# Layer A of a two-layer trunk: plain products for the in-projection, convolution and gate straight from PSUM

## The chip, the cores and the metric

The kernel runs on one core of one Trainium2 chip. Five engines work side by side: TensorE multiplies matrices (the profile writes PE, and PEld for its weight loads), VectorE (DVE), ScalarE (ACT) and GpSimd (POOL) work element by element, and SyncE (SP) issues most of the DMAs. Each engine runs its own instructions in order and waits on semaphores for the others. SBUF is the working memory of 128 partitions; matmuls write their results to PSUM, from where DVE or ACT fetch them.

The metric is the device time of one execution in microseconds (us), the median of several executions. The profile is of one further execution; its span runs from the first to the last instruction.

## The reference

The input x has 2048 tokens of 1024 features. Two layers follow, each `x <- x + mixer(rmsnorm(x))`, and a final norm. Layer A is a recurrent mixer, layer B a gated short convolution; both widen 1024 features to 1536 channels (12 heads of 128), with a SiLU gate beside them:

```python
def rg_lru(u, gate_w, gate_b, lam):
    g = sigmoid(einsum('bshi,hio->bsho', u by heads, gate_w) + gate_b)
    r, i = halves of g
    log_a = -LRU_C * r * softplus(-lam)
    a = exp(log_a)
    bterm = sqrt(-expm1(2 * log_a)) * (i * u)
    return h with h[t] = a[t] * h[t-1] + bterm[t]

def recurrent_mixer(h, w_in, conv_w, conv_b, gate_w, gate_b, lam, w_out):
    u = h @ w_in
    gate, xb = u[..., :WIDTH], u[..., WIDTH:]
    xb = causal_depthwise_conv(xb, conv_w, conv_b)     # 4 taps
    y = rg_lru(xb, gate_w, gate_b, lam)
    return (y * silu(gate)) @ w_out

def shortconv_mixer(h, w_in, conv_w, w_out):
    bg, cg, xv, gate = four parts of h @ w_in
    y = bg * causal_depthwise_conv(cg * xv, conv_w)    # 3 taps
    return (y * silu(gate)) @ w_out
```

(The code above is shortened from the reference.) Everything is float32.

## The kernel before

**Products.** A float32 product is made of three float16 matmuls (`mm3`, L475, L478 and L479 in the profile): operands are split into a high and a low half. For activations `add` does it (L280 on ACT, L282 on DVE, tiles `op`), for weights `split` inside the in-projection (L400 on ACT, L401 on DVE, tiles `wc`, eight buffers), and `OutProj.split` for the out-projections (L1029, L1030, tiles `zs` and `wf`). Products accumulate in PSUM in six tiles tagged `acc`; two more PSUM tiles, tagged `g`, hold gates and small sums. The split weights are scaled by a power of two, and `undo` takes the scale back at the eviction.

**Units.** The in-projection of a layer goes by units of 256 output channels (two heads, m = 0 and 1). Layer A has 12 units, two for each pair of heads: an x unit (the recurrent branch) and a g unit (the gate). Each unit runs over two halves of 1024 tokens, each of two chunks c of 512. A half-unit is a 2 by 2 block product: `unit` computes it by Winograd's scheme with seven products of 12 matmuls (PSUM tiles p, q and r), `unit_of_blocks` with eight. In layer A units 0 and 1 go by blocks (the first chunk of unit 0 even in float32, `first_blocks`), units 2 to 11 by Winograd, and so does all of layer B.

Winograd needs sums of operands: T1 to T4 of the activations (`build_sums`: L306 on POOL and DVE) and S1 to S4 of the weights (`wsum`: L452 on POOL), so a unit has seven split weight tiles. Its results come out one after another, each computed from an earlier one (`plus`, L514 on DVE; copies L524 and L540 on ACT). `unit_weights` is the preparation of the next unit's weights: load (L389), squares for the scale (L362), the scale itself (L371 to L380), then the splits. It is a generator that is advanced a step at a time between the products of the present unit (`pace`).

**The mixer of layer A** is a generator too, one for each pair, half and chunk, advanced from the list `side`. For each of the two heads: the convolution (first tap L761 on POOL or L757 on ACT, three more L768 on DVE) reads `xb` from SBUF, where three columns before the chunk were copied by `halos` (L195, L198). Two gate matmuls in float32 follow (L783, two records each), tanh (L787), exp and tanh (L794, L795), a square (L796), two products on DVE (L797, L800). One root over both heads (L806, which needs another activation table), then the product on POOL (L812), the scan on DVE (L813), its last column (L817), the product with the gate on POOL (L819, which makes z in the tile `sg`), the store of z to DRAM (L686) and its square for the scale of the out-projection (L690). The gate itself comes from the g unit: tanh (L845) and a DVE step (L848). `u`, `th`, the tanh tiles and `a` share nine buffers `e`.

**Order.** In a pair, x half 0, x half 1, g half 0 and g half 1 follow one another. The mixer of half 0, chunk 0 is started after x half 1, that of chunk 1 after g half 0, those of half 1 after g half 1; so a pair's mixers run while its g unit and the next pair's x unit are computed. For the last pair all but the first mixer are marked `late`: they have their own tiles and run inside the out-projection, held behind its products (`hold`). The final order on each engine is laid out by a scheduler before the run, from the order of the program, `tc.high_priority` and order-only edges (`after`).

**The out-projection** (`OutProj`) loads z back (`zr`), splits it, and computes each output tile from 12 heads. It begins with the first five pairs of chunk 0 (`EARLY`), so that the last pair has time.

**Layer B's gate** is tanh (L939), a DVE step (L940) and a product on POOL (L944); the factor 0.5 that this form of SiLU needs is put into the convolution's weights (`bwh`).

## Time and profile before

| | us |
|---|---|
| median of 3 runs | 2152.18 |
| lowest and highest | 2148.42, 2154.61 |
| profiled execution | 2150.58 |
| its span | 2148.8 |

The stages, read off PE's timeline: the start with units 0 and 1 up to 157.8 us; units 2 to 11 of layer A up to 686.75; the out-projection of layer A from 693.2 to 982.7; layer B from there, its out-projection in the last 270 us. A row of a group gives the line in the source, the engine, the operation, what it writes and reads, and after the bar its busy time in us, the mean ns of one, and the idle time of that engine just before it with what ended most of it.

### The profile page before, as it was taken

Reading aid. Unit: us, or ns where it says so; the run is one execution under the profiler, and the core shown is the slowest. Engines: PE = TensorE matmul, PEld = TensorE weight load, DVE = VectorE, ACT = ScalarE, POOL = GpSimd, SP = SyncE. Lnnn points to the kernel's source line nnn. Section 1 sums busy time; section 2 is a strip of 40 time slices with the busy share of each in tenths; the row PEclk is TensorE's granted clock in tenths of the full one; section 3 lists DMA queues with packets and bytes.
Section 4 is the critical chain, followed back from the end, with each engine's and each line's share of the span. In section 5 each row is a group of like instructions: output and inputs, shape, how many; then the busy total and the mean of one; then the engine's idle time right before and its main releaser. Section 6 shows DMA issues by size and latency. Waiting matters only on the chain.

```text
span 2148.8 us, 25164 instructions
## 1 busy us (share of the span) xinstructions
PE 1979.2 (92%) x9110; PEld 924.0 (43%) x9110; DVE 1375.4 (64%) x2058; ACT 997.1 (46%) x1833; POOL 809.0 (38%) x650
## 2 busy tenths in 40 slices
PE   7587898989788979998899999999999999999997
PEld 3232343434233434443344444444444444444467
DVE  8679787878668763747974653744736547465323
ACT  6456777776657563314343333342442332344221
POOL 3644453545433131325553342433442423313220
PEclk9798999999899989998999999999999999999999
DMA  5101121121311435442102112121120020193202
GB/s 190 43 5 45 59 74 64 60 89 45 104 48 50 167 129 131 167 108 69 41 29 89 40 35 79 34 74 42 43 98 30 33 81 5 66 346 132 85 23 71
DMA packets 94205, 167.74 MB, mean 78 GB/s; under 512 B 11456, under 2 KB 15168, under 8 KB 94080
## 3 DMA queue, kind: packets, MB, share of 16 engines
q1 hardware_dynamic: 93520, 164.82, 23.5%
q0 software_dynamic: 560, 1.32, 0.3%
q8 instruction: 71, 1.16, 0.2%
q14 instruction: 54, 0.44, 0.1%
HBM read 124.14 MB, written 41.96 MB: 77 GB/s over the span
## 4 chain that ended last, share of the span: by engine, by line
PE 61%; DVE 21%; ACT 8%; DMA 5%; issue 4%; POOL 1%; SPq 0%; DVEq 0%; ACTq 0%; POOLq 0%
PE acc L478 6%; PE acc L479 6%; PE acc L475 6%; PE q L479 6%; PE q L475 6%; PE q L478 6%; DVE u L768 4%; PE p L475 4%; PE p L478 4%; PE p L479 4%; PE r L479 4%; PE r L475 4%; PE r L478 4%; DVE tg L813 3%; DVE op L282 3%
## 5 line engine op out<-in xcount | busy, mean ns | idle before, releaser
L475 PE MATMUL q<-op,wc 128*128 128x512 f16 x816 | 310.8, 382 | 21.7 <-DVE xb L514 6.4
L475 PEld LDWEIGHTS <-wc 128*128 128x128 f16 x2016 | 201.6, 100 | 293.9 <-ACT wc L400 36.9
L479 PEld LDWEIGHTS <-wc 128*128 128x128 f16 x2016 | 199.6, 99 | 290.8 <-issue 55.4
L478 PEld LDWEIGHTS <-wc 128*128 128x128 f16 x2016 | 199.4, 99 | 273.1 <-issue 50.1
L475 PE MATMUL acc<-zs,wf 128*128 128x512 f16 (+1 forms) x864 | 304.1, 359 | 13.6 <-ACT zs L1029 10.4
L478 PE MATMUL acc<-zs,wf 128*128 128x512 f16 (+1 forms) x864 | 308.4, 357 | 4.5 <-DVE zs L1030 4.3
L478 PE MATMUL q<-op,wc 128*128 128x512 f16 x816 | 311.8, 382 | 0.4 <-DVE op L282 0.4
L479 PE MATMUL q<-op,wc 128*128 128x512 f16 x816 | 311.5, 382 | 0.0
L479 PE MATMUL acc<-zs,wf 128*128 128x512 f16 (+1 forms) x864 | 306.8, 357 | 0.0
L475 PE MATMUL p<-op,wc 128*128 128x512 f16 x544 | 209.2, 385 | 23.5 <-ACT wc L400 22.9
L475 PE MATMUL r<-op,wc 128*128 128x512 f16 x544 | 208.1, 383 | 9.8 <-ACT wc L400 6.5
L478 PE MATMUL r<-op,wc 128*128 128x512 f16 x544 | 208.1, 383 | 8.8 <-DVE op L282 8.8
L478 PE MATMUL p<-op,wc 128*128 128x512 f16 x544 | 209.2, 385 | 0.0
L479 PE MATMUL p<-op,wc 128*128 128x512 f16 x544 | 208.6, 384 | 0.7 <-DVE wc L401 0.7
L479 PE MATMUL r<-op,wc 128*128 128x512 f16 x544 | 207.4, 381 | 1.3 <-DVE fixed L817 1.2
L401 DVE SCALAR_TENSOR_TENSOR wc<-ws,fixed,wc 128x512 f16<-128x512 f32 x140 | 141.5, 1018 | 93.5 <-ACT wc L400 92.8
L217 POOL TENSOR_TENSOR sa<-sa,sq 128x512 f32<-128x512 f32 x70 | 99.9, 1428 | 213.6 <-ACT sq L216 145.6
L890 POOL TENSOR_TENSOR pb<-pb,cg 128x512 f32<-128x512 f32 x48 | 65.8, 1371 | 242.9 <-ACT pb L540 162.0
L452 POOL TENSOR_TENSOR ws<-wr 128x512 f32<-128x512 f32 x70 | 110.2, 1574 | 94.0 <-ACT pre L713 33.9
L768 DVE SCALAR_TENSOR_TENSOR u<-xb,fixed,u 128x512 f32<-128x512 f32 x144 | 129.8, 923 | 2.9 <-POOL u L761 2.8
L475 PEld LDWEIGHTS <-wf 128*128 128x128 f16 x864 | 85.4, 99 | 97.3 <-issue 9.8
L783 PE MATMUL pg<-u,gts 128*128 128x512 f32 x192 | 100.5, 633 | 24.0 <-DVE u L768 9.3
(188 smaller groups left out, 3269.5 us busy)
## 6 DMA issues: line engine op xcount, KB each, us to landing
wr<-in_wb SPq DMA_DIRECT2D x100, 256.0 KB, 3.2
xs<-in_xT SPq DMA_DIRECT2D x48, 256.0 KB, 5.7
zA<-sg SPq DMA_DIRECT2D x48, 256.0 KB, 2.0
zr<-zA SPq DMA_DIRECT2D x48, 256.0 KB, 5.3
zB<-ed SPq DMA_DIRECT2D x48, 256.0 KB, 2.0
zr<-zB SPq DMA_DIRECT2D x48, 256.0 KB, 5.3
wr<-in_wa SPq DMA_DIRECT2D x44, 256.0 KB, 3.6
xr<-x SPq DMA_DIRECT2D x32, 256.0 KB, 5.2
```

The lines of the kernel that those rows point to most:

```text
L217: squared[0] = eng.tensor_tensor(out=acc, in0=acc, in1=sq, op=ALU.add)
L282: return hi, v.tensor_tensor(out=t[:, 1, :], in0=src, in1=t[:, 0, :], op=ALU.subtract)
L401: v.scalar_tensor_tensor(out=t[:, 1, :], in0=src, scalar=sw[:, 2:3], in1=t[:, 0, :], op0=ALU.mult, op1=ALU.subtract,)
L452: g.tensor_tensor(out=t, in0=x, in1=y, op=op)
L475: ins = nc.tensor.matmul(acc, wh, xh, start=start, stop=False, **kw)
L478: nc.tensor.matmul(acc, wh, xl, start=False, stop=False, **kw)
L479: return nc.tensor.matmul(acc, wl, xh, start=False, stop=stop, **kw)
L768: v.scalar_tensor_tensor(out=u, in0=tap(k), scalar=wc(k), in1=u, op0=ALU.mult, op1=ALU.add)
L783: ins = nc.tensor.matmul(pg, gw[m][:, oo], u, start=True, stop=True)
L813: v.tensor_tensor_scan(out=y, data0=a, data1=w, initial=stA[:, h : h + 1], op0=ALU.mult, op1=ALU.add,)
L890: g.tensor_tensor(out=t, in0=t, in1=cg[m, half, c], op=ALU.mult)
```

## The change

1. **Plain products.** Units 2 to 11 of layer A go by `unit_of_blocks` too. `unit_weights` then makes four splits and no sums; `build_sums` and its calls are gone. Layer B stays with Winograd.
2. **Convolution from PSUM.** `unit_of_blocks` hands its accumulators to an `evict` function. For x units that is `conv`: ACT makes the last tap with the bias, DVE adds three shifted taps, all reading PSUM, and three columns are kept in a small `tail` tile for the next chunk, whose first columns get three small steps. There are no halos in layer A. The taps are scaled by `undo`. `u` takes one of the eight `xc` buffers.
3. **Gate from PSUM.** For g units `evict` is `silu`: tanh on ACT and one step on DVE, both reading PSUM, into `sg`.
4. **Mixers.** Those of a half start right after the x half. They have no convolution in them, work in place in `u`, and the `late` forms are gone: the last pair is treated like the others.
5. **z when both factors are there.** `gate` is called after the scan and after the silu; the later of the two makes z, on DVE instead of POOL, and issues its store. The square of z is emitted four steps later (`defer`, `tick`), behind the last product, into a tile of its own (`zjunk`); this holds for layer B too.
6. **Layer B's gate** is one `AF.Silu` on ACT; the DVE step and `bwh` go.

```diff
+        if plain:
+            for name, a in (("A11", a11), ("A21", a21), ("A12", a12), ("A22", a22)):
+                w[name] = split(a, sw)
+                yield
+            return
...
-    def unit_of_blocks(w, ops, dest, done, end, chunks=range(2)):
+    def unit_of_blocks(w, ops, dest, done, end, chunks=range(2), evict=None, pin=False):
...
+                        if pin:
+                            pe_last[0] = blocks_last[0]
                 if kh == 0:
+                    flush()
                     yield
             for m in range(2):
+                if evict:
+                    evict(m, c, accs[m], w["undo"])
+                    continue
...
-            take(n, 0, w, prep, False, pace=SCALE)
-            take(n, 1, w, prep, False)
+            take(n, 0, w, prep, plain(n), pace=[0, 0, 1, 0, 0] if plain(n) else SCALE)
+            take(n, 1, w, prep, plain(n))
...
+            def conv(m, half, c, a, undo=None):
+                h = heads[m]
+                us[m, half, c] = u = xct("u")[:, 0:CH]
...
+                with tc.high_priority(1000):
+                    s.activation(u, a, AF.Identity, scale=ac(3), bias=col(PC_AB + h))
+                    for n in range(1, 4):
+                        v.scalar_tensor_tensor(
+                            out=u[:, n:], in0=a[:, 0 : CH - n], scalar=ac(3 - n), in1=u[:, n:],
                             op0=ALU.mult, op1=ALU.add,
                         )
+                    v.tensor_scalar(
+                        out=tail[:, 0:3], in0=a[:, CH - 3 : CH],
+                        scalar1=1.0 if undo is None else undo, scalar2=None, op0=ALU.mult,
+                    )
+                    for n in range(1, 4) if before is not None else ():
                         v.scalar_tensor_tensor(
+                            out=u[:, 0:n], in0=before[:, 3 - n : 3], scalar=wc(3 - n),
+                            in1=u[:, 0:n], op0=ALU.mult, op1=ALU.add,
                         )
...
+            def gate(m, half, c):
+                if (m, half, c) in gated and (m, half, c) in scanned:
+                    z = sg[m, half, c]
+                    v.scalar_tensor_tensor(
+                        out=z, in0=us[m, half, c], scalar=gu[1], in1=z, op0=ALU.mult, op1=ALU.mult
+                    )
+                    store_z("A", hp, m, half, c, z)
+                    z_square(z, hp, m, half, c)
...
-                for m, (h, a, w, y, thi) in enumerate(kept):
-                    g.tensor_tensor(out=w, in0=w, in1=thi, op=ALU.mult)
+                for m, (h, a, w, u) in enumerate(kept):
+                    g.tensor_tensor(out=u, in0=w, in1=u, op=ALU.mult)
                     v.tensor_tensor_scan(
-                        out=y, data0=a, data1=w, initial=stA[:, h : h + 1],
+                        out=u, data0=a, data1=u, initial=stA[:, h : h + 1],
                         op0=ALU.mult, op1=ALU.add,
                     )
-                    v.tensor_copy(stA[:, h : h + 1], y[:, CH - 1 : CH])
-                    z = sg[m, half, c]
-                    g.tensor_tensor(out=z, in0=y, in1=z, op=ALU.mult)
-                    store_z("A", hp, m, half, c, z)
-                    z_square(z, y, hp, m, half, c)
+                    v.tensor_copy(stA[:, h : h + 1], u[:, CH - 1 : CH])
+                    scanned.add((m, half, c))
+                    gate(m, half, c)
...
             def xafter(half):
-                halos(xb, half, 3)
-                if half:
-                    side.extend([mixer(0, 0)] if hp else [mixer(1, 0), mixer(1, 1)])
-                    if hp == NH // 2 - 1:
-                        before_end(None)
+                side.extend([mixer(half, 0), mixer(half, 1)])
+                if half and hp == NH // 2 - 1:
+                    before_end(None)
...
+            def silu(m, half, c, a, undo):
...
+                sg[m, half, c] = t = sgt("sg")
+                with tc.high_priority(1000):
+                    s.activation(t, a, AF.Tanh, scale=gu[0][:, 0:1])
+                    v.scalar_tensor_tensor(
+                        out=t, in0=t, scalar=1.0, in1=a, op0=ALU.add, op1=ALU.mult
+                    )
                 gated.add((m, half, c))
+                gate(m, half, c)
...
             def gafter(half):
-                if half == 0:
-                    side.append(mixer(0, 1 if hp else 0))
-                    if hp == NH // 2 - 1:
-                        before_end(marks[-1])
-                else:
-                    side.extend([mixer(1, 0), mixer(1, 1)] if hp else [mixer(0, 1)])
+                if half == 0 and hp == NH // 2 - 1:
+                    before_end(marks[-1])
...
             def gdone(m, half, c, t):
                 th = et("th")
-                s.activation(th, t, AF.Tanh, scale=0.5)
-                v.scalar_tensor_tensor(
-                    out=th, in0=th, scalar=1.0, in1=t, op0=ALU.add, op1=ALU.mult
-                )
+                s.activation(th, t, AF.Silu)
```

`gu` holds half the unit's `undo` (for the tanh) and `undo` itself (for z), made by one small DVE step for each g unit.

More of the change, by code (lines that the diff above doesn't have):

```diff
@@ L143, in trunk @@
     gbh = keep(2 * NH)
-    bwh = keep(3 * NH)
     stA = keep(NH)
@@ L605, in first_done, with defer, tick @@
         return t
+    deferred = []
+    def defer(fn, steps):
+        deferred.append([steps, fn])
+    def tick(n=1):
+        for d in list(deferred):
+            d[0] -= n
+            if d[0] <= 0:
+                deferred.remove(d)
+                d[1]()
     def advance(side):
+        tick()
         while side and next(side[0], "end") == "end":
@@ L624, in take @@
         def take(n, half, w, prep, blocks, chunks=range(2), end=None, pace=None):
-            _, dest, done, before, after = units[n]
+            _, dest, done, before, after, *evict = units[n]
             before(half)
             pace = list(pace or ())
+            args = ()
+            if blocks:
+                take_out = evict and (lambda m, c, a, undo: evict[0](m, half, c, a, undo))
+                args = chunks, take_out, n > 1
             for _ in (unit_of_blocks if blocks else unit)(
                 w, ops[half], lambda m, c: dest(m, half, c), lambda m, c, t: done(m, half, c, t),
-                lambda: end(half) if end else after(half), *[chunks] * blocks
+                lambda: end(half) if end else after(half), *args
             ):
@@ L634, in take @@
                     next(prep, None)
-                for _ in range(1 + blocks + (l == 0 and half and n == len(units) - 1)):
+                for _ in range(1 + blocks):
                     advance(side)
@@ L638, in take, with plain @@
                 run(prep)
+        def plain(n):
+            return l == 0
         def start_blocks(w0, w1):
@@ L651, in ahead @@
             if n < len(units):
-                prep = unit_weights(l, units[n][0], w, behind=behind)
+                prep = unit_weights(l, units[n][0], w, behind=behind, plain=plain(n))
             next(prep, None)
@@ new lines, in conv, with wc, ac @@
+            def conv(m, half, c, a, undo=None):
+                h = heads[m]
+                us[m, half, c] = u = xct("u")[:, 0:CH]
+                if undo is not None and not taps:
+                    taps.append(cst.tile([P, 8], F32, tag="tap", name="tap", bufs=2))
+                    v.tensor_scalar(
+                        out=taps[0], in0=col(PC_AW + 8 * hp, 8), scalar1=undo, scalar2=None,
+                        op0=ALU.mult,
+                    )
+                def wc(k):
+                    return col(PC_AW + 4 * h + k)
+                def ac(k):
+                    return wc(k) if undo is None else taps[0][:, 4 * m + k : 4 * m + k + 1]
+                before = tails.get((m, 2 * half + c - 1))
+                tails[m, 2 * half + c] = tail = cst.tile([P, 4], F32, tag="tl", name="tl", bufs=8)
+                with tc.high_priority(1000):
[3 more added lines that the diff above has]
+                            out=u[:, n:], in0=a[:, 0 : CH - n], scalar=ac(3 - n), in1=u[:, n:],
@@ L776, in mixer @@
+            def mixer(half, c):
+                kept = []
                 for m in range(2):
-                    h = heads[m]
-                    u = us[m]
+                    if (half, c) == (0, 0):
+                        gw[m] = gate_weights(heads[m])
+                for m in range(2):
+                    h, u, w = heads[m], us[m, half, c], ws2[:, m, :]
                     th = []
@@ L807, in mixer @@
                 yield
-                yield
-                while any((m, half, c) not in gated for m in range(2)):
-                    yield
-                for m, (h, a, w, y, thi) in enumerate(kept):
-                    g.tensor_tensor(out=w, in0=w, in1=thi, op=ALU.mult)
+                for m, (h, a, w, u) in enumerate(kept):
+                    g.tensor_tensor(out=u, in0=w, in1=u, op=ALU.mult)
                     v.tensor_tensor_scan(
-                        out=y, data0=a, data1=w, initial=stA[:, h : h + 1],
+                        out=u, data0=a, data1=u, initial=stA[:, h : h + 1],
@@ L865, in in_A @@
+            def gafter(half):
+                if half == 0 and hp == NH // 2 - 1:
+                    before_end(marks[-1])
+            units.append((wa[2 * hp], xdest, nothing, beside, xafter, conv))
+            units.append((wa[2 * hp + 1], nothing, nothing, beside, gafter, silu))
         for hp in range(NH // 2):
@@ L1248, in second @@
         yield
-        behind = []
-        for ins in build_blocks(0, x1, inv1, hA[1]):
-            behind.append(ins[1])
-            yield
-        yield from build_sums(x0, hA[0], behind[NB])
+        yield from build_blocks(0, x1, inv1, hA[1])
     def ahead(l, wdram, sw=None):
```

114 lines of the change are left out of this document (31 added, 83 removed).

## The prediction

> **What bounds the kernel now.** I first read the page's engine totals and its 40 slices, to find the stages in which TensorE (PE) is not the limit.
>
> ```profile
> PE 1979.2 (92%) x9110; PEld 924.0 (43%) x9110; DVE 1375.4 (64%) x2058; ACT 997.1 (46%) x1833; POOL 809.0 (38%) x650
> ...
> PE   7587898989788979998899999999999999999997
> ...
> DVE  8679787878668763747974653744736547465323
> ...
> PEclk9798999999899989998999999999999999999999
> ```
>
> A slice is 53.7 us. From about slice 20 on PE is full, so layer B's in-projection and the last out-projection pay for matmuls alone. The holes are in the first 16 slices: layer A. I cut those stages with windows, at places taken from PE's timeline (the first product of unit 2, the last one of unit 11, the first and last matmuls of the out-projection).
>
> ```profile
> 157.80:688.60 530.80, 459.31 (x1871) 199.34 (x1869) 427.73 (x598) 368.65 (x637) 240.08 (x195) 0.95 0.20 64
> 693.20:982.70 289.50, 268.91 (x1213) 122.90 (x1213) 178.29 (x255) 125.30 (x216) 82.73 (x58) 0.96 0.45 135
> 982.70:1100.00 117.30, 100.75 (x448) 45.91 (x446) 102.29 (x145) 49.22 (x96) 65.12 (x48) 0.93 0.15 51
> ```
>
> The columns are span, then busy time of PE, weight load, DVE, ACT, POOL, then granted clock. In the 20 Winograd half-units (first row) PE is busy 459 of 531 us at a clock of 0.95, DVE 428. Next, PE's instruction groups in that window and, for the pace, its timeline.
>
> ```profile
> L475 PE MATMUL q<-op,wc 128*128 128x512 f16 x240 | 92.1, 384 | 12.2 <-DVE xb L514 6.4 <-DVE sg L514 5.7
> L783 PE MATMUL pg<-u,gts 128*128 128x512 f32 x168 | 84.4, 609 | 14.6 <-ACT wc L400 8.7 <-ACT th L845 2.9 <-DVE fixed L96 2.2
> L475 PE MATMUL p<-op,wc 128*128 128x512 f16 x160 | 62.9, 393 | 23.5 <-ACT wc L400 22.9 <-ACT sg L524 0.6
> L475 PE MATMUL r<-op,wc 128*128 128x512 f16 x160 | 62.7, 392 | 9.8 <-ACT wc L400 6.5 <-DVE fixed L817 3.3
> L478 PE MATMUL r<-op,wc 128*128 128x512 f16 x160 | 62.6, 391 | 8.8 <-DVE op L282 8.8
> ...
> L371 PE MATMUL pt<-fixed 128*128 128x4 f32 x18 | 2.5, 211 | 0.0
> ```
> ```profile
> 287.33 1.88 PE L783 MATMUL pg<-u,gts 128*128 128x512 f32 x4
> ...
> 686.75 1.88 PE L783 MATMUL pg<-u,gts 128*128 128x512 f32 x4
> 693.24 1.86 PE L475 MATMUL acc<-zs,wf 128*128 128x512 f16 x4 [4.61 <-ACT zs L1029]
> ...
> 949.67 0.38 PE L475 MATMUL acc<-zs,wf 128*128 128x512 f16 x1
> ...
> 965.85 0.38 PE L475 MATMUL acc<-zs,wf 128*128 128x512 f16 x1
> ```
>
> From the matmul at 949.67 to the one at 965.85 there are 75 starts: 16.18/75 = **0.2157 us** a matmul at full clock. A gate record (f32, two for each matmul) overlaps the next: (1.88 - 0.59)/3 = 0.43 us. So the in-projection, 157.8 to 686.75 = 529 us, holds 1680 x 0.2157 = 362 us of products, 168 x 0.43 = 72 us of gates and some 3 us of small matmuls: 438 us. **91 us are lost**: idle time, 71.5 us with the small groups not quoted, and about 20 us of lower clock behind it. The rows say what ended the idle time: weights (wc) 38.8 us with 0.7 in an unquoted row, evictions that a product accumulating on the same PSUM tile needs (xb, sg) 12.1, operands (op) 9.2. Only 11.4 us are anything else. DVE at 81% is late for all of these, but PE waits through them.
>
> **The change, part by part.** *Products.* A half-unit goes from 7 products of 12 matmuls to 8: +240 matmuls in the 20 half-units, 240 x 0.2157 = **+51.8 us** of PE. This cannot hide: PE is the busiest engine. With 184 gate records (the 8 that come before 157.8 stay there) the floor is 1920 x 0.2157 + 184 x 0.43 + 3 = 496 us.
>
> *Waits that go.* The plain unit splits four weight blocks and not seven, without the POOL sums, and takes 4 of the 8 wc buffers, so the next unit's four are made while this one runs: the 38.8 us on wc go. No product accumulates onto a tile that has been read half-way: the 12.1 us go. The operand sums T1 to T4 are not built any more: the 9.2 us on op go. The 11.4 us stay, with lower clock in their proportion, 20 x 11.4/71.5 = 3.
>
> *DVE, ACT and POOL.* These rows price the new work.
>
> ```profile
> L768 DVE SCALAR_TENSOR_TENSOR u<-xb,fixed,u 128x512 f32<-128x512 f32 x144 | 129.8, 923 | 2.9 <-POOL u L761 2.8
> ```
> ```profile
> L768 DVE SCALAR_TENSOR_TENSOR u<-xb,fixed,u x144: 718/744/1789, 91.9 to 763.9; 128x512 f32<-128x512 f32 x144
> ...
> L514 DVE SCALAR_TENSOR_TENSOR xb<-q,fixed,xb x30: 734/740/751, 196.2 to 661.1; 128x512 f32<-128x512 f32 x30
> ```
> ```profile
> L813 DVE TENSOR_TENSOR_SCAN tg<-a,fixed 128x512 f32<-128x512 f32 x40 | 73.1, 1830 | 3.0 <-POOL fixed L812 3.0
> ...
> L797 DVE SCALAR_TENSOR_TENSOR fixed<-fixed,tg 128x512 f32<-128x512 f32 x40 | 30.8, 770 | 21.5 <-ACT fixed L796 21.2
> ```
> ```profile
> L787 ACT ACTIVATE tg<-pg,fixed 128x512 f32<-128x512 f32 x82 | 53.1, 676 | 19.0 <-DVE fixed L817 6.4 <-PE q L479 6.3 <-PE p L479 3.6
> L794 ACT ACTIVATE a<-tg,fixed 128x512 f32<-128x512 f32 x41 | 33.2, 809 | 2.9 <-DVE tg L800 2.3 <-DMA zA<-sg 0.6
> ...
> L806 ACT ACT_TABLE_LOAD x20 | 25.7, 1283 | 0.3
> L690 ACT ACTIVATE tg<-sg 128x512 f32<-128x512 f32 x40 | 25.0, 624 | 86.3 <-DVE fixed L817 50.5 <-POOL sg L819 21.1 <-DVE fixed L96 13.0
> ...
> L806 ACT ACTIVATE fixed<-fixed 128x1024 f32<-128x1024 f32 x20 | 21.2, 1059 | 6.1 <-DVE fixed L797 6.0
> L400 ACT ACTIVATE wc<-wr,fixed 128x512 f16<-128x512 f32 x28 | 19.9, 711 | 14.3 <-DVE fixed L377 6.7 <-DVE tg L813 4.1 <-DVE sg L848 2.0
> ...
> L690 ACT ACTIVATION_READ_ACCUMULATOR tg<-sg 128x1 f32 x40 | 7.5, 188 | 0.0
> ...
> L757 ACT ACTIVATE u<-xb,fixed 128x512 f32<-128x512 f32 x4 | 3.2, 804 | 0.0
> ```
>
> The trace has no convolution from PSUM. The nearest row is the Winograd eviction (L514), which reads PSUM and one SBUF tile: 734 to 751 ns, never more. The present convolution (L768) reads two SBUF tiles: 744 ns at the median but up to 1789. I take 0.74 us; the other end, 0.92, is L768's mean. For 24 steps in a pair that is 4.4 us more of DVE.
>
> [...]
>
> For one pair of heads (four half-units, 97 us of PE) DVE then has 24 convolution steps x 0.74, 8 silu and 8 z products at 0.74, 16 mixer products at 0.77, 8 scans at 1.83, 8 splits near 0.8 and some 6 us of small columns: about 69 us, against 428 x 4/20 = 86 now. POOL keeps only the product before the scan. So DVE is not the bound on average.
>
> What is new is **crowding**. All mixers of an x half now run in the next half-unit: two in x half 1, two in g half 0, none in the others, where one per half-unit ran. ACT in x half 1: 8 gate tanh 5.4, 4 x (0.81 + 0.81 + 0.62) = 9.0, two roots 2.1, four table loads 5.1, 4 convolution starts at 0.8 = 3.2, 4 splits 2.8: 27.6 us. In g half 0: the same 21.6, plus 4 silu tanh 2.7, 8 squares with their accumulator reads 6.5: 30.8. Together 58.4 against PE's 2 x (96 x 0.2157 + 16 x 0.43) = 55.2. DVE, too, is full in x half 1: 12 convolution steps 8.9, 8 mixer products 6.2, 4 scans 7.3, 4 splits 3.2 and 3 of small columns, 28.6 against 27.6. ACT falls some 3 to 4 us behind in each pair and makes it up in g half 1. If PE waits for it, through the two gate PSUM tiles, that is 5 x 4 = 20 us; if the products go on, nothing. I take the middle, 10. So the in-projection loses 11.4 + 3 + 10 = 24 us: 496 + 24 = 520, **-9 us** against 529. Its bounds: 5 us lost (-28), and the present 91 (+58).
>
> *End of layer A.* Three of the last pair's four mixers now run inside the out-projection, on purpose held back. These are PE's groups in it.
>
> ```profile
> L478 PE MATMUL acc<-zs,wf 128*128 128x512 f16 x384 | 146.9, 383 | 4.5 <-DVE zs L1030 4.3
> ...
> L475 PE MATMUL acc<-zs,wf 128*128 128x512 f16 x384 | 142.6, 388 | 13.6 <-ACT zs L1029 10.4 <-DVE xr L1303 3.2
> L783 PE MATMUL pg<-u,gts 128*128 128x512 f32 x17 | 11.1, 782 | 7.0 <-DVE u L768 7.0
> ```
>
> From 686.75 to 982.7 are 296 us. 1152 x 0.2157 = 248.5, gates 17 x 0.43 = 7.3, small matmuls 5.7: 34.5 us are lost, 25 idle and the rest at low clock. After the change all mixers are done in g half 0, and z needs only the silu. The gates are counted above; the wait for u and for late z splits goes. What stays is the first wait, 4.6 + 1.2 us, and the cold clock behind it: I take 11 us in all. 265 against 296: **-31 us**; bounds 5 us lost (-37) and 30 (-12).
>
> *Start.* The last inverse norm lands here, and unit 2 begins there:
>
> ```profile
> 118.76 0.75 DVE L274 SCALAR_TENSOR_TENSOR xs<-xs,fixed,inv 128x512 f32<-128x512 f32 x1 [6.78 <-DMA inv<-rd]
> ```
> ```profile
> 157.83 0.38 PE L475 MATMUL p<-op,wc 128*128 128x512 f16 x1
> ```
>
> In these 39 us PE has 144 matmuls, 31 us, and a few gates. Without the operand sums about half the rest goes: **-3 us**, between -8 and +5, since more of pair 0's gates may fall there. Before 118 the chain is DMA and POOL squares, which the change leaves.
>
> *Layer B and the rest.* Silu saves 48 DVE steps under a PE that is full; I take -1 us, for the 983 to 1100 stretch, bounds 0 and -3. Deferred squares, the halo copies that go, and the tail columns lie beside PE: nothing; without that cover they belong to the crowding term. So do the head's gate weights: they are now asked for in the step whose matmul reads them, not two steps before.
>
> ```profile
> gts<-in_ga SPq DMA_DIRECT2D x12, 128.0 KB, 3.4
> ```
>
> If SP issues them no earlier, PE waits 3.4 us in each of five pairs, 17 us; I count nothing, since the slot of a head is free two pairs ahead and the order is laid out beforehand, and keep the 17 for the range. Weight loads and z stores share SP's queue; a store that waits for z holds the loads behind it, but a unit's load now has one whole unit (48 us) of slack.
>
> **Sum:** -9 - 31 - 3 - 1 = -44 us on a span of 2148.8. That execution took 2150.6; the median of the runs shown is 2152.2, so 2152 - 44 = **2108 us**.
>
> **The rivals.** (a) *Crowding in full*: PE waits the 20 us for ACT, wc waits stay at a third (13 us), and low clock behind them costs some 7 more. Lost 54 instead of 24: 2138. For it: ACT at 106% in two half-units of four. Against: the last wait before the products was rarely ACT's gates (2.9 us for th in the pg row). (b) *Everything hidden*: 5 us lost in the in-projection, 5 in the out-projection, start -8: 2108 - 19 - 6 - 5 = 2078. For it: layer B's in-projection, where PE is full at DVE's 40 to 80%. (c) *Slower*: the mixer chain (gate, exp, root, POOL product, scan) becomes the pace. u now lives from the convolution to z in eight buffers, a pair's full need; if four chains take longer than a pair of products, the next x half finds no u buffer, the six accumulators stay full and PE stops. Four chains in 97 us are 24 us each without cost; the forecast's pace is 520/20 = 26.0 us, and from 26.0 + 44/20 = 28.2 us a half-unit on, the whole gain is gone; with the present loss of 91 us the time is 2108 + 67 = 2175. For it: POOL's product now waits 92.1 us for the root (POOL group below). Against: what PE waited for was mostly not this, and in the second fence below a chain takes 17 us, from its first gate tanh at 513.02 to the end of its POOL products at 530.40.
>
> ```profile
> L812 POOL TENSOR_TENSOR fixed<-fixed,tg 128x512 f32<-128x512 f32 x38 | 56.4, 1504 | 101.3 <-ACT fixed L806 92.1 <-PE r L479 9.2
> ```
> ```profile
> 513.02 1.26 ACT L787 ACTIVATE tg<-pg,fixed 128x512 f32<-128x512 f32 x2
> ...
> 527.84 2.56 POOL L812 TENSOR_TENSOR fixed<-fixed,tg 128x512 f32<-128x512 f32 x2 [11.19 <-ACT fixed L806]
> ```
>
> **How the numbers follow.** Forecast 0.57 (its own range 2092 to 2125), (a) 0.17, (b) 0.15, (c) 0.11. The range 2080 to 2142 leaves out (c) and the outer edges. A measurement of this kernel tells about 0.3%, 6.5 us, from no change. Faster by more than that: 0.57 + 0.15 + most of (a) = 0.85; within: 0.05; slower: 0.10.
>
> **What would show it.** Right: the plain products of units 2 to 11 end about 520 us after they begin; no wait for wc above 10 us in all; convolution steps at 0.74 us with no 1.7 us cases; no gates in the out-projection, which takes about 265 us. Wrong: PE idle before gate records, or before acc products for want of u; table loads well above 48 in layer A; PE idle above 33 us in the in-projection, where its own saving is gone.

## The result and the profile after

| | before | after |
|---|---|---|
| median, us (4 runs each) | 2150.82 | 2075.07 |
| lowest and highest | 2148.42, 2154.61 | 2074.04, 2075.85 |
| span of the profiled execution | 2148.8 | 2073.5 |
| its granted clock | 0.967 | 0.984 |

After divided by before is 0.9646, with a 95% interval of 0.9629 to 0.9663: the kernel is 76 us faster. The forecast was 2108, the range 2080 to 2142. The direction was right, and so was the main reason: plain products take less time although they are more matmuls. But the gain is 1.7 times the 44 us that were forecast, and the time lies 5 us below the range: the terms for the loss that would stay, in the units and in the out-projection, were too large.

Engine totals and slices of after, from its page:

```profile
PE 2002.3 (97%) x9350; PEld 946.5 (46%) x9350; DVE 1194.3 (58%) x2047; ACT 962.6 (46%) x1756; POOL 567.2 (27%) x458
...
PE   6699999999999999988999999999999999999997
...
PEclk9899999999999999999999999999999999999998
```

The holes in the first 16 slices are gone. What is left is the start (two slices at 6), two slices at 8 where layer B begins, and the end. The stages, cut again at PE's first product of unit 2 (about 152 us), its last product of unit 11 (651.7) and the last matmul of the out-projection (904.3), by windows:

```profile
151.00:651.70 500.70, 495.86 (x2127) 225.10 (x2125) 338.04 (x677) 375.34 (x625) 54.85 (x45) 0.99 0.22 72
651.70:904.30 252.60, 252.60 (x1193) 117.12 (x1192) 133.92 (x189) 84.29 (x150) 63.07 (x44) 1.00 0.45 143
904.30:1050.00 145.70, 129.55 (x581) 59.00 (x580) 112.06 (x159) 60.49 (x118) 76.38 (x58) 0.94 0.13 41
```

PE is busy 495.86 of 500.70 us in the units at a clock of 0.99, and all of the 252.60 us of the out-projection at 1.00. The waits of PE in the units, which came to 71.5 us, are now two rows:

```profile
PE pg L820 <- ACT tg L824: 4.7, 1, 4.7
PE pt L722 <- ACT fixed L711: 0.2, 1, 0.2
```

| stage | before | after | measured | forecast |
|---|---|---|---|---|
| up to unit 2 | 157.8 | 152 | -6 | -3 |
| units 2 to 11 | 529 | 500 | -29 | -9 |
| to the end of the out-projection | 296 | 252.6 | -43 | -31 |
| layer B and the end | 1166.1 | 1169.2 | +3 | -1 |
| span | 2148.8 | 2073.5 | -75 | -44 |

Of the 31 us that the forecast lacked, 20 are in the units, 12 in the out-projection and 3 at the start; layer B took 4 back.

### The profile page after: what moved, and what is told of

Its sections match the earlier page's. It is cut to its first block, busy times and chain, and to the rows that moved or that the text cites. A ratio compares the mean times of both kernels' runs of the same rounds, so it can differ in the third digit from the quotient of the medians.

```text
span 2073.5 us, 25220 instructions
## 1 busy us (share of the span) xinstructions
PE 2002.3 (97%) x9350; PEld 946.5 (46%) x9350; DVE 1194.3 (58%) x2047; ACT 962.6 (46%) x1756; POOL 567.2 (27%) x458
## 4 chain that ended last, share of the span: by engine, by line
PE 80%; DVE 11%; DMA 3%; issue 3%; ACT 3%; POOL 1%; SPq 0%; DVEq 0%; ACTq 0%; POOLq 0%
PE acc L464 12%; PE acc L468 12%; PE acc L467 12%; PE q L468 6%; PE q L467 6%; PE q L464 6%; PE r L464 4%; PE p L468 4%; PE p L464 4%; PE p L467 4%; PE r L467 4%; PE r L468 4%; DVE op L280 3%; PE pg L820 2%; DVE xs L272 2%
## 5 line engine op out<-in xcount | busy, mean ns | idle before, releaser
L464 PEld LDWEIGHTS <-wc 128*128 128x128 f16 x2096 | 208.8, 100 | 277.6 <-issue 33.0
L468 PEld LDWEIGHTS <-wc 128*128 128x128 f16 x2096 | 206.2, 98 | 269.2 <-issue 25.9
L467 PEld LDWEIGHTS <-wc 128*128 128x128 f16 x2096 | 206.2, 98 | 265.0 <-issue 33.0
L464 PE MATMUL acc<-op,wc 128*128 128x512 f16 x752 | 283.7, 384 | 21.5 <-DVE sg L874 11.0
L467 PE MATMUL acc<-op,wc 128*128 128x512 f16 x752 | 287.1, 382 | 8.3 <-DVE op L280 8.2
L468 PE MATMUL acc<-op,wc 128*128 128x512 f16 x752 | 287.5, 382 | 2.9 <-DVE wc L385 2.9
L464 PE MATMUL q<-op,wc 128*128 128x512 f16 x576 | 218.4, 381 | 4.7 <-DVE pb L503 2.5
L468 PE MATMUL q<-op,wc 128*128 128x512 f16 x576 | 219.5, 381 | 0.0
L467 PE MATMUL q<-op,wc 128*128 128x512 f16 x576 | 219.2, 381 | 0.0
L845 POOL TENSOR_TENSOR u<-fixed,u 128x512 f32<-128x512 f32 x48 | 60.2, 1276 | 501.7 <-ACT fixed L842 501.7
L385 DVE SCALAR_TENSOR_TENSOR wc<-ws,fixed,wc 128x512 f16<-128x512 f32 x100 | 97.4, 975 | 98.3 <-ACT wc L384 98.3
L464 PE MATMUL p<-op,wc 128*128 128x512 f16 x384 | 146.3, 381 | 0.0
L467 PE MATMUL p<-op,wc 128*128 128x512 f16 x384 | 146.3, 381 | 0.0
L468 PE MATMUL p<-op,wc 128*128 128x512 f16 x384 | 146.0, 380 | 0.0
L468 PE MATMUL r<-op,wc 128*128 128x512 f16 x384 | 146.0, 380 | 0.0
L467 PE MATMUL r<-op,wc 128*128 128x512 f16 x384 | 146.0, 380 | 0.0
L464 PE MATMUL r<-op,wc 128*128 128x512 f16 x384 | 145.8, 380 | 0.0
```

Source lines behind the costliest of these rows:

```text
L385: v.scalar_tensor_tensor(out=t[:, 1, :], in0=src, scalar=sw[:, 2:3], in1=t[:, 0, :], op0=ALU.mult, op1=ALU.subtract,)
L464: ins = nc.tensor.matmul(acc, wh, xh, start=start, stop=False, **kw)
L467: nc.tensor.matmul(acc, wh, xl, start=False, stop=False, **kw)
L468: return nc.tensor.matmul(acc, wl, xh, start=False, stop=stop, **kw)
L845: g.tensor_tensor(out=u, in0=w, in1=u, op=ALU.mult)
```

## The experiments

Times are medians; the ratio is to the kernel before, run on the same chip. The kernel before took 2145 to 2149 us beside these runs (medians), so kernels are compared by ratio or on one chip.

| run | median us | ratio (95%) |
|---|---|---|
| e1_plain_only | 2089.37 | 0.9733 (0.9716 to 0.9749) |
| e6_plain_nolate | 2092.60 | 0.9749 (0.9724 to 0.9774) |
| e2_copy_first | 2072.85 | 0.9656 (0.9642 to 0.9671) |
| e3_mixers_later | 2072.34 | 0.9653 (0.9637 to 0.9669) |
| e12_more_steps | 2072.26 | 0.9650 (0.9635 to 0.9664) |
| e8_z_pool | 2074.25 | 0.9663 (0.9638 to 0.9688) |
| e4_tanh_b | 2070.39 | 0.9643 (0.9622 to 0.9664) |
| e5_act_3 | 2089.17 | 0.9735 (0.9719 to 0.9750) |
| e5_act_6 | 2119.90 | 0.9869 (0.9855 to 0.9884) |
| e7_wc14 | 2151.85 | 1.0024 (1.0011 to 1.0036) |
| e10_load_back | 2111.87 | 0.9831 (0.9817 to 0.9846) |
| e13_winograd_light | 2135.44 | 0.9919 (0.9898 to 0.9940) |
| e11_inv_pe | 2054.05 | 0.9561 (0.9545 to 0.9577) |
| e14_inv_pe_b | 2045.67 | 0.9510 (0.9494 to 0.9525) |
| e15_after_again | 2071.75 | 0.9631 (0.9616 to 0.9646) |

### Which part of the change carries the gain

**Plain products alone.** The kernel before with part 1 of the change and nothing else.

```diff
+        if plain:
+            for name, a in (("A11", a11), ("A21", a21), ("A12", a12), ("A22", a22)):
+                w[name] = split(a, sw)
+                yield
+            return
...
-            take(n, 0, w, prep, False, pace=SCALE)
-            take(n, 1, w, prep, False)
+            take(n, 0, w, prep, l == 0, pace=[0, 0, 1, 0, 0] if l == 0 else SCALE)
+            take(n, 1, w, prep, l == 0)
```

> The kernel before with one part of the change alone: units 2 to 11 of layer A by plain blocks (four weight splits, no operand or weight sums); convolution, gate, mixers and their places as before. Theory A (PE's losses in layer A came from the weight tiles, operand sums and Winograd's chained evictions, 60 of 71.5 us of idle time): PE waits in units 2 to 11 fall to about 10 to 15 us, these units take about 515 us against 529, the out-projection keeps its late mixers and its 296 us, the start gains 5; about 2130 us. Theory B (the losses came from DVE's load and the mixers' order, and Winograd only showed them): PE keeps 50 us or more of waits, the units take 550 us or more, 2165 us or more.

Measured: 2089.37 against 2146.37, so 57 us of the 76, and 41 below the 2130 of theory A. Its reason held, but the gain is larger on two counts: the units take 492 us (153.5 to 645.4) instead of its 515, and the out-projection, which it left at 296, takes 276. The last product of unit 11 starts at 645.2 us, 41 earlier than before (in after it is 35: seven us of the last pair's gates have moved ahead of it). The rest is lost between there and the end of the out-projection, which is at 921.5 and in after at 904.3. Windows of e1_plain_only, then of after, in the middle of that stage:

```profile
690.00:740.00 50.00, 38.25 (x152) 16.39 (x151) 40.36 (x63) 34.75 (x58) 18.68 (x13) 0.90 0.31 104
```
```profile
690.00:740.00 50.00, 50.00 (x239) 23.26 (x238) 27.95 (x46) 17.64 (x35) 10.30 (x8) 1.00 0.53 185
```

In 50 us e1 issues 152 matmuls and after 239: idle time, and a clock of 0.90 beside it. The waits of e1's PE in this stage are for z, for a gate operand and for the eviction of an output tile (`xr`):

```profile
PE acc L480 <- ACT zs L1035: 5.0, 1, 5.0
PE pg L789 <- DVE fixed L823: 3.3, 1, 3.3
PE acc L480 <- DVE xr L1308: 3.3, 1, 3.3
```

**Is it the `late` marks that e1 lacks?** e1 with the marks off, so that the last pair's mixers run like the others.

```diff
-                late = hp == NH // 2 - 1 and half + c > 0
+                late = False
...
-                if half and hp == NH // 2 - 1 and not last:
+                if False:
```

> The plain-products kernel (e1) with one thing more: the last pair's mixers are no longer marked late (no own tiles, no hold behind the out-projection's products, gates not put off). Theory A (what e1 lacks against the changed kernel, 14 us, lies in the held-back mixers of the last pair: PE at 0.8 clock and 12 us of waits between 700 and 750 us): 2072 to 2079 us. Theory B (it lies in the lighter mixers: conv and z from PSUM, in place, z on DVE): stays at 2085 to 2092 us.

It gains nothing (0.9749 beside 0.9733), as theory B had it. The marks are not what e1 lacks.

**Reading PSUM.** After, with the accumulators copied to SBUF by ACT first, so that convolution and gate read SBUF as before.

```diff
+                if undo is not None:
+                    t = et("xs")
+                    with tc.high_priority(1000):
+                        s.activation(t, a, AF.Copy, scale=undo)
+                    a, undo = t, None
```

> The changed kernel, but ACT first copies each accumulator to SBUF, and convolution and gate read SBUF. Nine tenths of the order is kept. Theory A (PE is the bound with room on ACT and DVE): 16 copies of 0.68 us more ACT for each pair of heads, some DVE steps back at 1.7 us beside POOL, PE still without waits: 2075 to 2080 us. Theory B (reading PSUM directly is what keeps DVE and ACT below the limit): ACT at 87 of 97 us in a pair and later evictions, PE waits 3 us or more in each pair: 2090 us or more.

**The mixers' places, and the number of their steps.** After, with each mixer started where the kernel before starts it (e3), and that with three more empty steps in each (e12).

```diff
-                side.extend([mixer(half, 0), mixer(half, 1)])
...
+                if half:
+                    side.extend([mixer(0, 0)] if hp else [mixer(1, 0), mixer(1, 1)])
...
+                if half == 0:
+                    side.append(mixer(0, 1 if hp else 0))
...
+                else:
+                    side.extend([mixer(1, 0), mixer(1, 1)] if hp else [mixer(0, 1)])
```

> The changed kernel with the mixers at the places of the kernel before: one in g half 0, one in g half 1, two in the next x half 0; those of the last pair's second half run beside the out-projection. Theory A (the early mixers of the last pair are what freed the out-projection): units 2 to 11 end at most 7 us earlier, since gates move out of them, the out-projection has PE waits again, 10 to 25 us; 2085 to 2100 us. Theory B (the out-projection was freed by plain products and lighter engines alone, the place matters nothing): 2073 to 2078 us. Theory C (two mixers in one half-unit cost PE time): faster than 2070 us.

> The kernel with short mixers at the old places (e3) with three empty steps put into each mixer, so that it takes as many steps of the surrounding loop as in the kernel before. Theory A (e1's lost 14 us are the length of the mixers in steps: the last ones end too far into the out-projection): PE waits and low clock return in the first 100 us of the out-projection, 2080 to 2092 us. Theory B (they come from the work itself: gate, convolution and z in separate operations): 2070 to 2076 us.

**z on POOL, and layer B's gate by tanh.** After with one of these undone at a time.

```diff
-                    v.scalar_tensor_tensor(
-                        out=z, in0=us[m, half, c], scalar=gu[1], in1=z, op0=ALU.mult, op1=ALU.mult
-                    )
+                    g.tensor_tensor(out=z, in0=us[m, half, c], in1=z, op=ALU.mult)
```
```diff
-                s.activation(th, t, AF.Silu)
+                s.activation(th, t, AF.Tanh, scale=0.5)
+                v.scalar_tensor_tensor(
+                    out=th, in0=th, scalar=1.0, in1=t, op0=ALU.add, op1=ALU.mult
+                )
```

> The changed kernel with z made on POOL (one product of two SBUF tiles) in place of DVE; the factor undo in z is left out, so the output is another one. Theory A (POOL beside DVE's two-input steps slows both, and that was part of the loss before): scans and mixer steps get cases near 2 us, DVE's busy time in layer A does not fall although 48 steps leave it, and the time is 2080 us or more. Theory B (there is room): 2072 to 2078 us.

> The changed kernel with layer B's gate as before (tanh, a DVE step, halved convolution weights). Theory A (layer B is bound by PE, the DVE step is hidden): within 4 us of the changed kernel, 2071 to 2079 us. Theory B (the DVE step counts at the start of layer B, where DVE is full): 2080 us or more.

All five lie at 0.9643 to 0.9663 beside 0.9646 and 0.9631 for after itself, and each time is that of the theory by which the part does not matter, or up to 2.2 us below it. None of these parts is needed by itself; two of them undone together were not run. Of theory A for e8 half came true: the scans did get slow cases (last section), but PE did not wait for them. Nor is the wait for z alone what e1 lacks: e12 waits 7.8 us for it too, but its first product of the out-projection is at 635.4 us, 16 before that of after (7 of these are gates that it runs later), so it had gained ahead of that place what it loses there. What is left between e1 (0.9733) and after is what all five have in common: mixers without a convolution of their own, in place in `u`, with z made when both factors are there and its square put off. These were not taken apart further; which detail of them brings the last 16 to 19 us stays open.

### Why Winograd cost more than its matmuls saved

**Was it a lack of weight tiles?** Of the 71.5 us of waits before, 38.8 had wc as releaser. The kernel before with 14 tiles instead of 8:

```diff
-pair16(wp, "wc", "wc", 8)
+pair16(wp, "wc", "wc", 14)
```

> The kernel before with 14 weight tiles wc in place of 8, nothing else. Theory A (the shortage of wc tiles made the weight waits, 38.8 us of PE idle time): these fall below 10 us, units 2 to 11 take about 490 us against 529, 2110 us or less. Theory B (the seven splits and the POOL sums themselves come too late behind DVE and POOL, whatever the number of tiles): weight waits stay above 25 us, 2135 to 2150 us.

The theory of a tile shortage fell: the time is 0.24% longer. Waits of PE from 158 to 682 us, the largest rows:

```profile
PE q L475 <- DVE xb L514: 11.0, 5, 4.6
PE pg L783 <- DVE u L768: 10.5, 5, 5.1
PE r L478 <- DVE op L282: 8.6, 2, 7.8
PE q L475 <- DVE fixed L817: 7.8, 1, 7.8
PE p L475 <- ACT wc L400: 5.5, 2, 4.7
```

wc fell from 38.8 us to 5.7 (one row not shown), and evictions and u took its place; all rows sum to 61.6, where they came to 71.5 before. Those 10 us of waits did not shorten the time. The name at the end of a wait told which of several late things came last.

**Is it the load, or the order in which things depend on each other?** Two runs from the two sides. e10 is e1 with dummy steps on DVE, ACT and POOL for those that Winograd needed more, whose results no product reads (the sums T1 to T4 are not among them). e13 is before with Winograd and all its dependences, but with two of four convolution taps left out.

```diff
+                t = buf(wp, "ws", "ws", 2)
+                g.tensor_tensor(out=t, in0=a11, in1=a, op=ALU.add)
+                if name != "A11":
+                    s.activation(ajunk, t, AF.Copy, scale=sw[:, 2:3])
+                    v.scalar_tensor_tensor(
+                        out=vjunk, in0=t, scalar=sw[:, 2:3], in1=t, op0=ALU.mult, op1=ALU.subtract
+                    )
...
+                for _ in range(1 + (m + c == 0) if pin else 0):
+                    v.scalar_tensor_tensor(
+                        out=vjunk, in0=accs[m], scalar=w["undo"], in1=d, op0=ALU.mult, op1=ALU.add
+                    )
```
```diff
-                    for k in range(1, 4):
+                    for k in range(1, 2):
```

> The plain-products kernel (e1) with idle work put back on the engines, about what Winograd's form had more: in units 2 to 11 five DVE steps reading PSUM in each half-unit (as its five evictions), and in each unit four sums on POOL and three further splits (ACT and DVE) of them, results unused; no product waits for any of it, and no more weight tiles. Theory A (load: DVE, ACT and POOL were too full and late for everything, which Winograd's extra work made): units 2 to 11 go back from about 490 to 520 us or more, 2120 us or more. Theory B (dependences: PE waited because Winograd's products need chained evictions and seven tiles in order): PE stays without waits, 2089 to 2100 us.

> The kernel before, Winograd and all, with two of the convolution's four taps left out (96 DVE steps, about 88 us of DVE in layer A; the output is another one). It is the counterpart of e10: load taken away, dependences kept. Theory A (DVE's load is what makes Winograd's chained evictions and splits late): PE waits in units 2 to 11 fall from 71 to 35 us or less, 2110 us or less. Theory B (the dependences cost by themselves): waits stay above 55 us, 2135 us or more.

The same 500 us of the units in four kernels, by windows: before, e13, e10, e1.

```profile
140.00:640.00 500.00, 432.69 (x1776) 187.97 (x1775) 399.67 (x556) 347.02 (x603) 237.50 (x191) 0.95 0.19 62
```
```profile
140.00:640.00 500.00, 437.22 (x1777) 191.42 (x1775) 355.99 (x486) 347.33 (x600) 234.44 (x193) 0.94 0.21 65
```
```profile
140.00:640.00 500.00, 479.31 (x2038) 215.55 (x2037) 394.83 (x558) 373.29 (x644) 214.13 (x195) 0.99 0.21 68
```
```profile
140.00:640.00 500.00, 493.59 (x2131) 223.80 (x2130) 307.53 (x440) 372.27 (x637) 169.84 (x161) 1.00 0.22 70
```

Before and e10 load DVE alike (400 and 395 us) and POOL nearly so (238 and 214), yet PE is busy 433 us in the one and 479 in the other. And with 44 us less of DVE, e13 has PE at 437, hardly above before. Load put back costs 21 us in the whole time (e10 against e1, by the ratios), between the bounds of both theories. It is not quite free of dependences: the dummy steps read accumulators, and PE waited for them to give these back:

```profile
PE acc L488 <- DVE fixed L595: 5.1, 2, 3.7
```

Taking load off DVE and keeping the dependences gives 14 to 17 us (e13, by the medians and by the ratio), which is theory B's: its units keep 65 us of waits, where before had 71.5. So of the 57 us some 21 at most are load. The larger part is, by subtraction, what e10 did not put back, above all seven products whose accumulation, eviction and operands wait for one another; no run takes that part to pieces. In e13 the waits are named u, evictions and wc:

```profile
PE pg L783 <- DVE u L768: 18.0, 7, 6.8
PE q L475 <- DVE sg L514: 9.4, 6, 3.0
PE q L475 <- DVE fixed L817: 8.7, 3, 7.4
PE r L475 <- ACT wc L400: 7.5, 1, 7.5
```

### Was there crowding?

After, with three or six extra squares on ACT for each head and chunk of a mixer, by the expectation 12.5 or 25 us in a pair of some 97.

```diff
                     s.activation(w, a, AF.Square)
+                    for _ in range(3):
+                        s.activation(zjunk, a, AF.Square)
```

> The changed kernel with three squares more on ACT in each head and chunk of a mixer (144 in all, results unused), about 1.6 us each time, 12.5 us for a pair of heads. Theory A, the prediction's crowding (PE waits when ACT has more to do in x half 1 and g half 0 than these two half-units last): 58.4 + 12.5 against 55.2, 15 us or more in each pair, 60 to 80 us in all, 2135 to 2155 us. Theory B (only a whole pair has to balance, gates slip into g half 1): ACT 88 of 97 us, no PE waits beyond 5 us, 2075 to 2082 us.

> The changed kernel with six squares more on ACT in each head and chunk of a mixer, 25 us for a pair of heads (three gave +14 us in all). Theory A (a pair must balance: ACT 76 + 25 = 101 us against PE's 97, and three already lay near that edge): 2110 to 2125 us. Theory B (each further us on ACT beside the mixers is paid in full from the point where three began to cost: 12.5 us more in each of five pairs): 2145 us or more.

On their own chips, e5_act_3 is 16.6 us above the mean of e2 and e3, between its two theories, and e5_act_6 47.9 above the mean of e12 and e15, within theory A of its own. Windows of after, e5_act_3 and e5_act_6:

```profile
140.00:640.00 500.00, 495.16 (x2123) 224.80 (x2122) 339.16 (x676) 375.74 (x627) 54.86 (x45) 0.99 0.22 73
```
```profile
140.00:640.00 500.00, 482.62 (x2048) 217.40 (x2046) 322.05 (x651) 426.64 (x727) 53.08 (x43) 0.99 0.21 71
```
```profile
140.00:640.00 500.00, 464.16 (x1953) 207.01 (x1952) 308.55 (x608) 468.99 (x814) 51.63 (x40) 0.98 0.22 70
```

With ACT busy 75% of the time PE idles 5 us of 500, at 85% 17, at 94% 36. In e5_act_6 the largest wait is the one that the prediction looked for, a gate product for the tanh that frees its PSUM tile:

```profile
PE pg L820 <- ACT tg L824: 19.1, 5, 5.9
```

So the mechanism of crowding is real, but after stands short of its edge. Its one wait of 4.7 us, at 223.37 us in g half 0 of units 2 and 3, is for the same tanh, though there ACT itself stood still: the root, which waited for DVE, was ahead of that tanh in ACT's queue.

```profile
220.25 1.06 ACT L842 ACTIVATE fixed<-fixed 128x1024 f32<-128x1024 f32 x1 [2.62 <-DVE fixed L834]
```

The other four pairs have none. ACT's timeline in the pair of units 4 and 5 (a half-unit is 25 us, so g half 0 runs from about 302 to 327 and g half 1 to 352), shows where the work went that did not fit:

```profile
330.72 1.06 ACT L842 ACTIVATE fixed<-fixed 128x1024 f32<-128x1024 f32 x1
331.80 1.28 ACT L824 ACT_TABLE_LOAD   x1
333.09 0.69 ACT L824 ACTIVATE tg<-pg,fixed 128x512 f32<-128x512 f32 x1
...
355.17 1.06 ACT L842 ACTIVATE fixed<-fixed 128x1024 f32<-128x1024 f32 x1
```

One root of the pair is at 330.7, in g half 1, and the last at 355.2, in the next pair's first half. The mixers slide into the two half-units that have none of their own, while PE goes on with products.

### What is left, and a version that beats both

In after the first 150 us still hold the widest holes. Timeline of DVE, then of PE:

```profile
77.18 0.18 DVE L234 RECIPROCAL r<-r 128x4 f32<-128x4 f32 x1 [0.88 <-ACT r L233]
92.88 1.41 DVE L272 SCALAR_TENSOR_TENSOR xs<-xs,fixed,inv 128x512 f32<-128x512 f32 x2 [15.52 <-DMA inv<-rd]
94.21 0.68 DVE L874 SCALAR_TENSOR_TENSOR sg<-sg,acc 128x512 f32<-128x512 f32 x1
```
```profile
94.95 0.61 PE L464 MATMUL acc<-op,wc 128*128 128x512 f16 x1 [10.95 <-DVE sg L874]
```

The inverse norm r is ready at 77.4 and reaches all partitions through a DMA at 92.9. The step that waits for it stands at the head of DVE's queue; behind it stands the gate's step, which needs nothing but DVE and frees an accumulator, and PE waits 10.95 us for that one. e11 spreads this norm with PE, through a matmul and a copy on ACT, which the kernel does elsewhere already. e14 does the same at the end of layer A, where layer B's first norms go by POOL's DMA.

```diff
-            inv_of(acc, inv1[c], sp)
+            inv_of(acc, inv1[c])
```
```diff
-        inv_of(sums[c], inv[c // 2][c % 2], g if c in (0, 2) else None)
+        inv_of(sums[c], inv[c // 2][c % 2])
```

> The changed kernel with the inverse norms of the second 1024 tokens spread over the partitions by PE and an ACT copy, as for the first, in place of two DMAs through DRAM, which take some 15 us each at the start. Theory A (those DMAs hold DVE, and behind it the gate's eviction, for which PE waits 11 us at 84 to 95 us): units 2 to 11 begin 8 to 15 us earlier, 2060 to 2067 us. Theory B (the squares' sums on POOL end too late anyway): 2070 to 2077 us.

> The kernel with the norm spread by PE at the start (e11), and the same for the norms of the out-projection's chunks 0 and 2 in layer A, in place of their DMAs from POOL's queue. Theory A (the wait at the start of layer B, 7 us for the sum on POOL and the clock behind it, has the same kind of cause): 2040 to 2050 us. Theory B (that wait is for POOL's sum of squares of the last chunk, which no DMA delays): 2051 to 2058 us.

DVE's timeline in e11_inv_pe at the same place:

```profile
78.86 0.18 DVE L234 RECIPROCAL r<-r 128x4 f32<-128x4 f32 x1 [0.88 <-ACT r L233]
79.07 0.87 DVE L244 TENSOR_SCALAR dg<-fixed,r 128x128 f32<-128x128 f32 x4
81.35 1.28 DVE L874 SCALAR_TENSOR_TENSOR sg<-sg,acc 128x512 f32<-128x512 f32 x2 [1.41 <-ACT sg L873]
```

The gate's step now runs at 81.35 instead of 94.21. e11 is 17.7 us faster than after on the same chip (2054.05 beside e15's 2071.75), or 15 by the ratios, more than the one wait of 10.95. Theory A held, with a time below its 2060. Windows of the 40 us around it, after and then e11_inv_pe, show that the clock rises as well, from 0.86 to 0.97, and that 58 more matmuls start:

```profile
60.00:100.00 40.00, 26.01 (x113) 11.50 (x112) 23.50 (x27) 15.88 (x29) 12.12 (x8) 0.86 0.12 33
```
```profile
60.00:100.00 40.00, 36.74 (x171) 17.93 (x170) 37.23 (x59) 28.08 (x49) 13.80 (x9) 0.97 0.10 27
```

e14 brings 8 more (11 by the ratios), as theory A had it: after's largest wait at the start of layer B is gone from it.

```profile
PE ss L221 <- POOL sa L215: 7.5, 1, 7.5
```

With 2045.67 us, 0.951 of before (0.9494 to 0.9525), e14 is the best of the study. The run of after beside it:

> The changed kernel itself, on the same chip as the two beside it, so that e11, e14 and it can be set side by side: 2070 to 2077 us.

It gave 0.9631, inside the interval of its first runs.

## Why the prediction was right, and where it was wrong

- **Right: plain products pay although they add 51.8 us of PE.** The floor of 496 us for the units was right: after takes 500. The gain is the 91 us of loss before, of which after keeps about 5. e1 shows that this part alone carries 57 of the 76 us.
- **Right by the sum, wrong by the rows: "the 38.8 us on wc go", "the 12.1 us go", "the 9.2 us on op go".** They went, but not each for its own reason, as the prediction put it. e7 took 33 of the 38.8 us of wc waits away alone and nothing was gained.
- **The step that failed first: "the 11.4 us stay, with lower clock in their proportion".** Of such waits 0.2 us are left (the other row, of 4.7 us, is counted to crowding below), and the 3 us of clock are not seen either (0.99 in the units). That is 14 of the 20 us by which the units were mis-sized. The step treated each wait as the property of its last releaser. In e7 the names trade places while most of the sum stays, which suggests that these waits were part of the same chain and went with it; no run shows this for them alone.
- **The term that failed beside it: crowding, 10 us, "the middle" between 20 and nothing.** It is 4.7 us at most, the one wait at 223.37 us. The working compared ACT's 58.4 us with PE's 55.2 in two half-units and took a shortage there for a loss in every pair. The balance that counts is that of the pair, since the work can slide; e5 finds the loss growing from 75% of ACT, where after stands, to 85%.
- **The out-projection: "what stays is the first wait ... I take 11 us in all".** Nothing stays: 252.6 us against 265, and all matmuls at full clock (1.00). The gates and late z left it, as said, and the first wait, taken over from the row of before, went as well. But their leaving was not needed for it. e1 keeps the old mixers there and still comes down from 296 to 276 us, with a wait for z (5.0 us) and the clock of 0.90 behind it. e3 has the last pair's late mixers back in this stage, with 16 gate records, some 7 us at 0.43, and some 3 us are lost:

```profile
643.99:906.39 262.40, 261.46 (x1212) 120.94 (x1211) 155.64 (x232) 111.31 (x190) 68.23 (x48) 0.99 0.46 146
```

- **Start: -6 for -3,** within its bounds. **Layer B: +3 for -1,** outside them but within what runs of one kernel differ by (2148.4 to 2154.6 for before); e4 shows no gain from silu that can be measured.
- **The counted nothings held.** No wait for the gate weights appears in after, so the 17 us kept for them were not needed. In all of layer A there are 56 table loads where there were 54.
- **The convolution from PSUM.** It was priced at 0.74 us a step and measured at 0.741 (the median of 138 steps, last section). e2 copies to SBUF first, and its 2072.85 us stand beside 2072.34 for e3 without copies on the same chip: here the copies neither gain nor cost.
- **The rivals and the range.** What happened is rival (b), everything hidden: 2078 was worked out and 2075 measured, with -8, -28, -37 and -1 for the stages where -6, -29, -43 and +3 came. Its evidence, that layer B's units keep PE full with DVE at 40 to 80%, was better than the half-unit count held against it. The range was drawn 2 us above this rival, to leave out "outer edges"; a case given 15 in 100 should have been inside. Rival (c), the mixer chain as the pace, did not appear.

## What to carry to other kernels

Sort waits by stage and take their sum as the quantity; the name behind a wait says who came last, not who would have to be faster, and removing one name may only bring up the next (e7: the waits for wc fell from 38.8 to 5.7 us, and the time rose by 0.24%). When work is moved, compare an engine's load with the bound over the time within which the work can slide, not over the piece where it is issued; a few dummy instructions there measure how far the edge is (after and the two of e5: PE idle 5 us of 500 with ACT at 75%, 17 at 85%, 36 at 94%). Look in an in-order queue for an instruction that waits for a DMA with a PSUM eviction behind it: here a one-line edit at such a place gave 15 to 18 us.

## What the hardware showed that was not expected

The steps of one line, the convolution's, in the trace of after: 138 with one input in PSUM and one in SBUF, and 6, in the first pair, with both in SBUF.

```profile
L783 DVE SCALAR_TENSOR_TENSOR u<-acc,tap,u x138: 721/741/751, 100.5 to 607.6; 128x511 f32<-128x511 f32 x46, 128x510 f32<-128x510 f32 x46, 128x509 f32<-128x509 f32 x46
L783 DVE SCALAR_TENSOR_TENSOR u<-xb,fixed,u x6: 742/750/1748, 42.9 to 52.3; 128x511 f32<-128x511 f32 x2, 128x510 f32<-128x510 f32 x2, 128x509 f32<-128x509 f32 x2
```

With a PSUM input none takes above 751 ns; of the six from SBUF two take 1605 and 1748, near the 1789 of the kernel before, and those two alone ran beside a POOL instruction (by start and end times). None of the 138 did, so these rows do not show what a PSUM input does beside POOL. The evictions of before do (L514, one input in PSUM and one in SBUF): 161 of 340 ran beside a POOL instruction, and none took above 752 ns. Of the 144 convolution steps of before, with two inputs in SBUF, 76 ran without POOL and took at most 752 ns; of the 68 beside it 32 took more than 1 us. In these counts all 34 steps above 1 us had both inputs in SBUF and ran beside a POOL instruction. The 144 steps took 132.9 us of DVE in before, 108.8 in after and 110.1 in e2, which reads copies in SBUF and has 3 of 144 steps above 1 us. So most of the saving, the 22.8 of 24.1 us that e2 has too, does not come from PSUM; it goes with the POOL work that is no longer beside these steps (beside 68 of 144 in before, 2 in after).

The scan reads two SBUF inputs too, and its median fell from 1836 to 1277 ns. Its rows in before, after and e8, which puts z back on POOL:

```profile
L813 DVE TENSOR_TENSOR_SCAN tg<-a,fixed x42: 1250/1836/2295, 162.9 to 696.1; 128x512 f32<-128x512 f32 x42
```
```profile
L846 DVE TENSOR_TENSOR_SCAN u<-a,fixed,u x48: 1266/1277/2277, 129.3 to 646.2; 128x512 f32<-128x512 f32 x48
```
```profile
L844 DVE TENSOR_TENSOR_SCAN u<-a,fixed,u x48: 1267/1918/2285, 127.9 to 647.7; 128x512 f32<-128x512 f32 x48
```

What counts is whether POOL runs at that moment: in after 18 of the 48 scans ran beside a POOL instruction and took 2266 to 2277 ns, the other 30 took 1266 to 1280. In e8 29 ran beside one. How busy POOL is in all says less: in e1 it is busy 170 us of the 500 where before has 238, yet 41 of 48 scans ran beside it.
